# Moving the second out-projection's blocks beside the first top-k search, the latent projections beside attention, and the late scores behind it

## The chip, the cores and the metric

The kernel runs on one core of one Trainium2 chip. The metric is the device time of one execution in microseconds (us), lower is better, as the median of several runs. Five engines work in parallel, each through its own instruction queue in order: TensorE (PE: matmuls; PEld: its weight loads), VectorE (DVE), ScalarE (ACT), GpSimd (POOL) and SyncE (SP, which here only issues DMAs). POOL issues some DMAs too. They wait for each other by semaphores.

## The reference, cut to what matters

Two blocks run one after the other on x of 1024 positions x 1024 features. The first has a gated convolution mixer and a dilated attention mixer and ends in a norm. The second is the part that the change reorders:

```
h   = rmsnorm(x) * (1 + scale) + shift
c_q, c_kv, k_idx, w_idx = split(h @ w_in)            # 256 + 256 + 64 + 8 columns ("latents")
score = sum_h w_idx[h] * relu(q_idx[h] @ k_idx)      # per query over all earlier keys
sel   = top 256 keys of each query by score
o     = softmax(q_lat @ c_kv[sel] + bias) @ c_kv[sel] # 8 heads
x = x + gate * (o @ w_uv @ w_o)
x = x + gate2 * conv_ffn(norm(x))                    # 2816 hidden features
out = rmsnorm(x)
```

The top 256 are found as a mask: a bitwise search for the 256th largest score of each query, then -1e30 is added to what lies below. Attention is computed densely under that mask. Queries 0 to 255 need no search, since they have at most 256 keys.

## The kernel before, in words

The 1024 positions are two chunks (c = 0, 1) of 512. Activations lie with features on the partitions, so a tile is 128 x 512. Every float32 product is three matmuls, since each operand is split into a high and a low part (hi x hi, hi x lo, lo x hi): a block of 128 output features from 1024 inputs is 8 x 3 = 24 matmuls of 128x512 (`gemm`).

The Python function `emit` writes the program as generators that are stepped in an order written by hand: `take(gen, n)` steps one n times, `drive` runs it out, `alternate` steps several in turn, and `Steps` wraps one so that it can be stepped now and then (`go`) and finished (`finish`). A list scheduler then places the instructions on each engine's queue, in about the order written, and moves later work ahead where an engine would otherwise stand still. `tc.issue_after` pins instructions behind a given one. The order of each queue is therefore fixed when the program is built.

The stages around the change, in the order of before:

- **Out-projection of layer 1** (`finish_layer1`, two generators `ends1[0]`, `ends1[1]`, one per chunk): 8 blocks (k = 0 to 7) of 24 matmuls each, whose raw weights are split on ACT and POOL (L377, L378) and whose results DVE adds to x (L683); then the statistics of the norm (L419, L427, a broadcast matmul into PSUM) and its application on DVE (L448, L451), ACT and POOL (L385), which gives H2 of that chunk. Before, six of chunk 1's eight blocks are issued ahead of `project(0)` (`take(ends1[1], 6)`), so they stand while chunk 0's norm is applied.
- **`project(c)`**: four latent blocks and one block of 72 columns, each of 24 matmuls, then 24 matmuls for the indexer's queries: 144 matmuls. DVE splits parts of the results (L1147, L1170), norms them (L1120) and so on. Its weights come ready-made from DRAM (L372) into `wring`, three slots that all weights share.
- **`scores(t)`** for query tiles t of 128 queries. Each head and each piece of up to 512 keys takes two matmuls into one PSUM bank, a relu on ACT (L1231) and a multiply-add on DVE (L1233 for head 0, L1236 for the others). t = 2, 3 come early. t = 4 to 7 are `late_scores`: 64 pieces, with the relu's result in two buffers (`ring`) and their PSUM in the tag `mm`, which has three banks at that point and serves `keys` and the out-projections too.
- **`topk`**, the search: 32 counts per tile, on DVE (L1268) or ACT (L1265), each followed by small decisions on DVE (L1274, L1277, L1288), then the mask (L1299 to L1314, POOL L1316, L1318). The *first search* (tiles 3 on DVE and 2 on ACT) is stepped beside the last two blocks of chunk 1's out-projection, `keys(0)` and `project(1)`. The *second search* (4, 5 on DVE; 6, 7 on ACT) is pinned behind the last DVE and ACT instructions of chunk 0's attention and runs beside `finish_dsa(0)` and `ffn_in(0)`.
- **`keys(c)`**: 16 tiles of 6 matmuls, each split by ACT (L1180) and DVE (L1181) and stored (L1182).
- **`attention(0, masks)`**: per head a query (L1349, L1350) with keys and values loaded by POOL-issued DMAs (L1353, L1354), four logit tiles (DVE L1395 adds the mask and takes the maximum, ACT L1400 the exponential, DVE L1402, L1403 the normalisation), then transposes on PE (L1420), split by ACT L1424 and DVE L1425, and the product with the values (ACT L1439). Logits and transposes use the PSUM tag `ps`. In the text written, the scores of tiles 4, 5 come ahead of it and 6, 7 behind it.
- **`finish_dsa(0)`**: chunk 0's last out-projection (8 blocks), its norm, and behind it **`ffn_in(0)`**: 44 blocks of 24 matmuls, that cover the second search on PE, then run beside `attention(1)`.

The lines that the change touches are:

```
        take(ends1[1], 6)
        for gen in ends1[1], keys(0), project(1):
                for _ in range(min(left, 4)):
        late_scores((4, 5))
        searches = [Steps(topk(sc[0:2])), Steps(topk(sc[2:4], True))]
        attention(0, masks)
        late_scores((6, 7))
```

Of the kernel before, what the change touches and what calls it, by code (L numbers as in the profile page):

```python
# [200 lines left out]
def emit(tc, I, OUT):  # L201
# [14 lines left out]
    with sp as sp, pp as pp, dp as dp:  # L216
# [266 lines left out]
        def alternate(*gens):  # L483
            gens = [iter(g) for g in gens]
            while gens:
                for g in list(gens):
                    try:
                        next(g)
                    except StopIteration:
                        gens.remove(g)  # L490
# [8 lines left out]
        def take(gen, n):  # L499
            for _ in range(n):  # L500
                next(gen)
# [564 lines left out]
        take(ends1[0], 5)  # L1066
        load_y(yscr, Yc, 1)
        drive(ends1[0])
        take(ends1[1], 6)

        banks["ps"].append(banks["mm"].pop(0))
        banks["po"].append(banks["mm"].pop(0))
# [372 lines left out]
                dma(yscr2[h, :, CH(c)], y.f)  # L1445
            y.free()

        def attention(c, masks):

            state = {}  # L1450
            query = lambda h: head_query(c, h, state) if h < HEADS else ()
            front = lambda h: head_front(c, h, masks, state) if h < HEADS else ()
            if c == 0:
                for h in range(LOOK):
                    drive(query(h))
                drive(front(0))
                for h in range(HEADS):
                    alternate(front(h + 1), head_back(c, h, state), query(h + LOOK))
            else:
                drive(query(0))  # L1460
                drive(front(0))
                for h in range(HEADS):
                    alternate(chain(query(h + 1), front(h + 1)), head_back(c, h, state))
            for i in range(2):
                for b in cq[i][c]:
                    b.free()
# [130 lines left out]
            qs[h][0].free()  # L1597
        search = [Steps(topk(sc[1:])), Steps(topk(sc[:1], True))]
        left = 32
        for gen in ends1[1], keys(0), project(1):  # L1600
            for _ in gen:
                for _ in range(min(left, 4)):
                    left -= 1
                    for x in search:
                        x.go()
# [1 line left out]
            for x in search:  # L1607
                x.go()
        masks = {3: search[0].value[0], 2: search[1].value[0]}
        sc = [ar.new(128 * (t + 1)) for t in (4, 5, 6, 7)]  # L1610
        ring = [ar.new(512) for _ in range(2)]

        def late_scores(ts):
            for t in ts:
                drive(scores(t, "mm", sc[t - 4], ring))
            if 7 in ts:
                for h in range(HEADS):
                    qs[h][1].free()
                for b in [kh, kl] + ring:
                    b.free()  # L1620

        late_scores((4, 5))
        searches = [Steps(topk(sc[0:2])), Steps(topk(sc[2:4], True))]

        attention(0, masks)
        late_scores((6, 7))
        rest = keys(1)
        take(rest, 8)
# [40 lines left out]
```

## Time and profile before

| | us |
|---|---|
| three runs | 2771.68, 2781.21, 2783.33 |
| their median | 2781.21 |
| the profiled execution's own time | 2774.49 |
| its span in the profile | 2772.8 |
| PE busy | 2604.5 (94%) |
| DVE busy | 1520.8 (55%) |
| ACT busy / POOL busy | 1123.9 / 1011.4 |

PE is the engine with the most work, so the share of busy time says little by itself: what matters is where PE stands still or runs at the lower of its two clocks, and which engine it then waits for. All times of the trace are counted from the start of the span. A "busy" figure of a stretch counts the time in which at least one instruction ran; instructions of one engine overlap a little at their ends, so the durations of single ones add up to more.

### The profile page before, as it was taken

What the parts mean: (1) busy time and instruction counts of PE and PEld (TensorE: products, weight loads), DVE (VectorE), ACT (ScalarE), POOL (GpSimd) and SP (SyncE); (2) the same over time, 40 slices, a digit from 0 to 9 for tenths busy, and PEclk for the clock granted to TensorE, in tenths of its full rate; (3) what the DMA queues carried; (4) which work ended last, traced back from release to release, by engine and by line L of the source; (5) the groups of instructions that cost most, each with busy time, mean ns of one, the idle gap of its engine ahead of it and who ended that gap; (6) DMA issues with size and microseconds to landing.
All of it is one profiled execution on the core that took longest, in us unless ns stands there. A gap on an engine that the chain in (4) does not pass through costs nothing. (4 is left out here: it accounts for less than half of the span.)

```text
span 2772.8 us, 34023 instructions
## 1 busy us (share of the span) xinstructions
PE 2604.5 (94%) x12070; PEld 2144.7 (77%) x12070; DVE 1520.8 (55%) x3260; ACT 1123.9 (41%) x1936; POOL 1011.4 (36%) x770
## 2 busy tenths in 40 slices
PE   8998998879999999999989887899999999999998
PEld 7876886658888888888778766778788777888887
DVE  7787223332666656756666598899655541222211
ACT  4211224323455455545443556775434433111132
POOL 1122335414465356545536335221311155200053
PEclk9999999989999999999999989999999999999999
DMA  7477228854444444444335573687566664576632
GB/s 290 164 266 244 82 89 313 302 193 136 172 176 151 168 161 174 145 175 170 132 120 172 194 253 111 211 259 251 205 210 206 236 200 121 195 257 243 234 117 73
DMA packets 208582, 524.67 MB, mean 189 GB/s; under 512 B 22258, under 2 KB 82202, under 8 KB 192796
## 3 DMA queue, kind: packets, MB, share of 16 engines
q1 hardware_dynamic: 199052, 497.20, 52.0%
q0 software_dynamic: 9216, 25.17, 3.0%
q8 instruction: 95, 1.56, 0.2%
q14 instruction: 75, 0.61, 0.1%
q10 hardware_dynamic: 144, 0.14, 0.0%
HBM read 394.03 MB, written 129.97 MB: 189 GB/s over the span
## 5 line engine op out<-in xcount | busy, mean ns | idle before, releaser
L256 PE MATMUL p<-page,wring 128*128 128x512 f32 (+2 forms) x8586 | 2027.1, 394 | 66.3 <-ACT page L384 8.5
L256 PEld LDWEIGHTS p<-page,wring 128*128 128x128 f32 (+1 forms) x8586 | 1605.0, 190 | 417.5 <-issue 12.5
L256 PE MATMUL p<-page,page 128*128 128x512 f32 (+5 forms) x2811 | 587.5, 351 | 81.5 <-ACT page L384 19.7
L256 PEld LDWEIGHTS p<-page,page 128*128 128x128 f32 (+1 forms) x2811 | 465.6, 199 | 168.7 <-ACT page L384 21.1
L378 POOL TENSOR_TENSOR wring<-wraw,wring 128x1024 fp32r<-128x1024 f32 (+1 forms) x159 | 390.4, 2457 | 512.1 <-ACT wring L377 508.3
L377 ACT ACTIVATE wring<-wraw 128x1024 fp32r<-128x1024 f32 (+1 forms) x159 | 164.7, 1037 | 333.0 <-PE p L256 292.1
L385 POOL TENSOR_TENSOR page<-page,page 128x512 fp32r<-128x512 f32 (+1 forms) x87 | 130.7, 1510 | 402.7 <-ACT page L384 382.6
L384 ACT ACTIVATE page<-page 128x512 fp32r<-128x512 f32 (+1 forms) x136 | 86.7, 651 | 222.3 <-DMA page<-d 96.7
L736 POOL TENSOR_TENSOR page<-page,page 128x512 f32<-128x512 f32 x96 | 124.7, 1303 | 115.8 <-ACT page L735 113.9
L355 DVE TENSOR_TENSOR wraw<-wraw,page 128x1024 fp32r<-128x1024 f32 (+1 forms) x64 | 83.1, 1298 | 105.2 <-ACT page L354 85.2
L301 DVE SCALAR_TENSOR_TENSOR page<-page,page 128x1024 f32<-128x1024 f32 x88 | 114.0, 1295 | 33.4 <-DMA page<-wmod 33.0
L745 POOL TENSOR_TENSOR page<-page,page 128x512 fp32r<-128x512 f32 x64 | 103.8, 1623 | 62.1 <-ACT page L744 61.9
L1541 DVE SCALAR_TENSOR_TENSOR page<-p,page,page 128x512 f32<-128x512 f32 (+1 forms) x17 | 12.2, 719 | 201.9 <-PE p L256 201.9
L743 DVE TENSOR_TENSOR page<-page 128x512 f32<-128x512 f32 x64 | 95.4, 1492 | 25.6 <-POOL page L736 25.6
L738 DVE TENSOR_TENSOR page<-p,page 128x512 f32<-128x512 f32 x96 | 66.2, 689 | 78.3 <-ACT page L735 73.0
L354 ACT ACTIVATE page<-wraw 128x1024 fp32r<-128x1024 f32 (+1 forms) x64 | 67.3, 1052 | 86.1 <-DMA wraw<-w3i 36.6
L1265 ACT ACTIVATE page<-page,page 128x1024 bf16<-128x1024 f32 (+1 forms) x93 | 86.7, 933 | 32.4 <-DVE page L1288 29.0
L441 POOL TENSOR_TENSOR page<-page,page 128x512 f32<-128x512 f32 x40 | 54.6, 1365 | 98.2 <-ACT page L440 98.2
L744 ACT ACTIVATE page<-page 128x512 fp32r<-128x512 f32 x64 | 57.1, 892 | 76.0 <-DVE page L743 75.9
L1375 POOL TENSOR_TENSOR page<-page,page 128x256 f32<-128x256 f32 x64 | 47.8, 759 | 107.2 <-DMA d<-page 35.1
L734 ACT ACTIVATE page<-p 64x512 f32<-64x512 f32 x96 | 57.3, 596 | 70.3 <-PE p L256 46.1
L1268 DVE TENSOR_SCALAR_CACHE_REDUCE page<-page,page 128x768 bf16<-128x768 f32 (+1 forms) x93 | 81.5, 876 | 1.5
(213 smaller groups left out, 2273.4 us busy)
## 6 DMA issues: line engine op xcount, KB each, us to landing
wring<-d SPq DMA_DIRECT2D x122, 1024.0 KB, 5.4
d<-page SPq DMA_DIRECT2D x95, 512.0 KB, 3.1
page<-wmod SPq DMA_DIRECT2D x88, 512.0 KB, 4.3
d<-page SPq DMA_DIRECT2D x153, 256.0 KB, 4.2
d<-wraw SPq DMA_DIRECT2D x63, 512.0 KB, 3.3
page<-d SPq DMA_DIRECT2D x121, 256.0 KB, 3.2
wraw<-w1i SPq DMA_DIRECT2D x56, 512.0 KB, 3.3
wraw<-w3i SPq DMA_DIRECT2D x44, 512.0 KB, 3.5
```

Of the source, the lines that this page charges most:

```text
L256: lastn["mm"] = T.matmul(out, lhsT=l, rhs=r, start=start, stop=stop)
L301: V.scalar_tensor_tensor(w.f, w.f, 1.0, sil[j // 6].f, op0=OP.mult, op1=OP.mult, accum_out=m)
L355: V.tensor_sub(raw.r[:, :n], raw.f[:, :n], hi.f[:, :n])
L377: A.activation(hi.r[:, :n], raw.f[:, :n], AF.Copy)
L378: (lo_engine or G).tensor_sub(lo.r[:, :n], raw.f[:, :n], hi.f[:, :n])
L384: A.activation(hi.r[:, :n], src, AF.Copy)
L385: (engine or V).tensor_sub(lo.r[:, :n], src, hi.f[:, :n])
L736: G.tensor_mul(sw.f, sw.f, rope[1].f[:, CH(c)])
L743: V.tensor_tensor(a.f, a.f, sw.f, op=OP.add)
L745: G.tensor_sub(out[1], shape(a.f), out[2])
L1265: A.activation(junk.b[:, 0:sc.n], sc.f, AF.Sign, scale=-1.0, bias=at, accum_out=one)
L1268: V.tensor_scalar(junk.b[:, 0:sc.n], sc.f, at, None, op0=OP.is_ge, op1=OP.add, accum_out=one)
```

## The change

It changes four things in the order in which the program is written, and no computation:

1. `take(ends1[1], 2)` in place of 6: only two of chunk 1's out-projection blocks stand ahead of `project(0)`, and six behind it.
2. The first search is stepped beside those six blocks and `keys(0)`, twice per step of these instead of four times. `project(1)` is no longer in that list.
3. `project(1)` is handed to `attention(0)`, which steps it once after each head and then finishes it.
4. `late_scores((4, 5))` and the creation of the second search move behind `attention(0)`, next to `late_scores((6, 7))`.

```diff
-        take(ends1[1], 6)
+        take(ends1[1], 2)
...
-        def attention(c, masks):
+        def attention(c, masks, beside=None):
...
                 for h in range(HEADS):
                     alternate(front(h + 1), head_back(c, h, state), query(h + LOOK))
+                    beside.go()
+                beside.finish()
...
         left = 32
-        for gen in ends1[1], keys(0), project(1):
+        for gen in ends1[1], keys(0):
             for _ in gen:
-                for _ in range(min(left, 4)):
+                for _ in range(min(left, 2)):
...
         masks = {3: search[0].value[0], 2: search[1].value[0]}
-        sc = [ar.new(128 * (t + 1)) for t in (4, 5, 6, 7)]
-        ring = [ar.new(512) for _ in range(2)]
...
+        attention(0, masks, Steps(project(1)))
+        sc = [ar.new(128 * (t + 1)) for t in (4, 5, 6, 7)]
+        ring = [ar.new(512) for _ in range(2)]
         late_scores((4, 5))
         searches = [Steps(topk(sc[0:2])), Steps(topk(sc[2:4], True))]
-
-        attention(0, masks)
         late_scores((6, 7))
```

The scheduler turns this into queues. In the rows below, a line is "line, operation, what is written <- what is read, shape"; p_N is a PSUM tile, page_N a buffer, wring the weights.

**First place: PE's queue where chunk 0's norm is applied.** p_10550 is block k = 1 of chunk 1's out-projection, p_10583 block k = 2; p_10466 and p_10463 are the broadcasts of chunk 0's norm; p_10601, p_10628 and p_10674 are the first blocks of `project(0)`, which read H2 of chunk 0 (page_474, page_9764, ...). Before:

```order
L256 MATMUL p_10550<-page_3236,wring 128x512
L256 MATMUL p_10583<-page_1401,wring 128x512
L256 MATMUL p_10583<-page_3228,wring 128x512
L256 MATMUL p_10583<-page_1401,wring 128x512
L256 MATMUL p_10583<-page_1685,wring 128x512
L256 MATMUL p_10583<-page_3236,wring 128x512
L256 MATMUL p_10583<-page_1685,wring 128x512
L256 MATMUL p_10583<-page_9768,wring 128x512 x3
L256 MATMUL p_10583<-page_9769,wring 128x512 x2
L256 MATMUL p_10466<-page_10144,page_65 128x512
```

After the change:

```order
L256 MATMUL p_10550<-page_3236,wring 128x512
L256 MATMUL p_10466<-page_10144,page_65 128x512
L256 MATMUL p_10586<-page_9832,page_65 8x384
L256 MATMUL p_10463<-page_10137,page_65 128x512
L256 MATMUL p_10601<-page_474,wring 128x512
L256 MATMUL p_10628<-page_474,wring 128x512
L256 MATMUL p_10674<-page_474,wring 72x512
L256 MATMUL p_10601<-page_474,wring 128x512 x2
L256 MATMUL p_10601<-page_9764,wring 128x512 x3
L256 MATMUL p_10601<-page_6107,wring 128x512
```

The four blocks k = 2 to 5 (96 matmuls) that stood from here on are gone from this place, and three blocks that need the norm's results follow directly, interleaved.

**Second place: DVE's queue at the end of chunk 1's out-projection.** L683 takes a block's result, L1018 is its square sum, L1236 a score of tile 2 or 3, L1268 a count of the first search. Before, block k = 7 (p_11111):

```order
L1236 SCALAR_TENSOR_TENSOR page_9833<-page_10999,page_4249,page_9833 128x384
L683 SCALAR_TENSOR_TENSOR page_10184<-p_11111,page_65,page_10184 128x512
L1236 SCALAR_TENSOR_TENSOR page_11008<-page_11022,page_4249,page_11008 128x512
L1017 TENSOR_TENSOR page_10327<-page_10327,page_2664 128x512
L1018 SCALAR_TENSOR_TENSOR page_10327<-page_2664,page_65,page_10327 128x512
```

After the change, block k = 6 (p_11103):

```order
L683 SCALAR_TENSOR_TENSOR page_10867<-p_11103,page_65,page_10867 128x512
L1282 TENSOR_SCALAR page_4249<-page_4249 128x1
L1277 TENSOR_SCALAR page_4249<-page_4249 128x1
L1268 TENSOR_SCALAR page_9305,page_4249<-page_10876,page_4249 128x512
L1288 SCALAR_TENSOR_TENSOR page_4249<-page_4249 128x1
L1018 SCALAR_TENSOR_TENSOR page_10327<-page_10867,page_65,page_10327 128x512
L1274 TENSOR_SCALAR page_4249<-page_4249 128x1
```

Counts of the search now stand between the blocks. In the whole queue, ten of the 32 counts on DVE stand ahead of the first L448 of chunk 1's norm (none before), 23 ahead of the last L1181 of `keys(0)` (16 before), and the last is followed directly by attention.

**Third place: PE's queue at the scores of tiles 4 to 7.** L1420 are attention's transposes; what reads page_261 and page_2871 (the indexer's keys) is a score. Before, in the middle of attention:

```order
L256 MATMUL p_12763<-page_261,page_11457 128x512
L256 MATMUL p_12763<-page_2871,page_11457 128x512
L1420 MATMUL p_12354<-page_65,page_11815 128x128
L256 MATMUL p_12257<-page_10919,page_9764 128x384
L1420 MATMUL p_12354<-page_65,page_11796 128x128
L256 MATMUL p_12768<-page_261,page_11457 128x384
L256 MATMUL p_12768<-page_2871,page_11457 128x384
L256 MATMUL p_12773<-page_261,page_9769 128x512
L256 MATMUL p_12773<-page_2871,page_9769 128x512
L256 MATMUL p_12257<-page_10919,page_9764 128x384 x2
```

After the change, behind the last product of attention (p_12548):

```order
L256 MATMUL p_12548<-page_12145,page_10335 128x256 x2
L256 MATMUL p_12548<-page_12145,page_9764 128x256
L256 MATMUL p_12614<-page_261,page_1685 128x256
L256 MATMUL p_12614<-page_2871,page_1685 128x256
L256 MATMUL p_12619<-page_261,page_11434 128x384
L256 MATMUL p_12619<-page_2871,page_11434 128x384
L256 MATMUL p_12624<-page_261,page_11434 128x256
L256 MATMUL p_12624<-page_2871,page_11434 128x256
```

From here on 59 score tiles stand on PE's queue one behind the other with nothing between them, and the first eight tiles of `keys(1)` and then `finish_dsa(0)` behind those. On DVE's queue all 56 late L1236 stand behind attention's last L1425, with 14 counts of the second search among them and 4 more among the first eight L1181 of `keys(1)`; before, six counts stood ahead of the eighth of these L1181. Of `project(1)`, two latent blocks and the 72-column block stand ahead of attention's first transpose, the rest among its heads.

## Rows read from the trace of the kernel before

**Rows 1.** Page, part 2: busy tenths in 40 equal slices of the span

```profile
PE   8998998879999999999989887899999999999998
DVE  7787223332666656756666598899655541222211
PEclk9999999989999999999999989999999999999999
```

**Rows 2.** Stretches of the span by engine; header names the columns

```profile
core 0: us, PE busy (x) PEld busy (x) DVE busy (x) ACT busy (x) POOL busy (x), PEclk, DMA share, GB/s
...
1523.30:1585.70 62.40, 59.47 (x262) 47.21 (x261) 32.40 (x62) 30.82 (x58) 17.09 (x13) 0.95 0.56 203
1585.70:1621.90 36.20, 22.95 (x84) 17.22 (x83) 35.23 (x111) 27.24 (x59) 16.22 (x12) 0.76 0.73 245
1621.90:1662.50 40.60, 35.81 (x161) 27.53 (x160) 37.24 (x137) 21.64 (x51) 11.89 (x15) 0.96 0.73 248
1662.50:1777.00 114.50, 96.09 (x455) 75.09 (x454) 98.48 (x302) 76.45 (x181) 51.78 (x80) 0.91 0.41 123
1777.00:1854.50 77.50, 67.36 (x284) 54.32 (x283) 70.95 (x202) 59.37 (x106) 15.17 (x12) 0.95 0.90 292
1854.50:1946.00 91.50, 91.50 (x403) 75.91 (x403) 84.37 (x231) 51.69 (x87) 19.61 (x18) 0.99 0.68 229
1946.00:2206.00 260.00, 252.40 (x1263) 211.08 (x1262) 147.01 (x400) 113.02 (x193) 47.53 (x78) 1.00 0.65 219
```

**Rows 3.** PE in order of time, from chunk 0's norm on

```profile
1493.84 17.84 PE L256 MATMUL p<-page,wring 128*128 128x512 f32 x76
...
1531.81 2.88 PE L256 MATMUL p<-page,wring 128*128 128x512 f32 x8 [2.71 <-DMA wring<-d]
```

**Rows 4.** DVE in order of time: chunk 0's norm, first and last

```profile
1494.45 3.38 DVE L448 SCALAR_TENSOR_TENSOR page<-page,page,p 128x512 f32<-128x512 f32 x5 [2.41 <-PE p L256]
...
1509.71 0.74 DVE L451 SCALAR_TENSOR_TENSOR page<-page,page,page 128x512 fp32r<-128x512 f32 x1
```

**Rows 5.** PE in order of time: chunk 1's norm

```profile
1592.86 2.93 PE L256 MATMUL p<-page,wring 128*128 128x512 f32 x6 [4.91 <-DVE page L1274]
1603.94 4.86 PE L256 MATMUL p<-wring,page 128*128 128x512 f32 x12 [8.15 <-DVE page L1181]
```

**Rows 6.** DVE in order of time: two counts of the first search, its end

```profile
1616.20 0.75 DVE L1268 TENSOR_SCALAR_CACHE_REDUCE page<-page,page 128x512 bf16<-128x512 f32 x1
...
1617.37 0.75 DVE L1268 TENSOR_SCALAR_CACHE_REDUCE page<-page,page 128x512 bf16<-128x512 f32 x1
...
1650.67 0.75 DVE L1268 TENSOR_SCALAR_CACHE_REDUCE page<-page,page 128x512 bf16<-128x512 f32 x1
...
1662.05 0.75 DVE L1314 SCALAR_TENSOR_TENSOR page<-page,page,page 128x512 f32<-128x512 f32 x1
```

**Rows 7.** DVE groups of the stretch 1662.5 to 1777: busy, mean ns, idle before

```profile
L1236 DVE SCALAR_TENSOR_TENSOR page<-page,page,page 128x512 f32<-128x512 f32 (+2 forms) x56 | 40.7, 737 | 0.5 <-ACT page L1231 0.5
L1395 DVE CUSTOM_DVE_ANT_0 page<-p,page 128x256 f32<-128x256 f32 (+1 forms) x47 | 16.9, 374 | 6.7 <-PE p L256 4.0 <-POOL page L1375 2.5
...
L1350 DVE SCALAR_TENSOR_TENSOR page<-p,page 128x512 fp32r<-128x512 f32 x6 | 4.1, 686 | 5.1 <-ACT page L1349 5.1
L1233 DVE TENSOR_SCALAR page<-page,page 128x512 f32<-128x512 f32 (+2 forms) x8 | 4.0, 509 | 0.0
...
L1170 DVE TENSOR_TENSOR page<-p,page 64x512 fp32r<-64x512 f32 x2 | 1.4, 688 | 0.1
L1181 DVE TENSOR_TENSOR page<-p,page 128x512 fp32r<-128x512 f32 x2 | 1.4, 684 | 0.0
```

**Rows 8.** ACT group of the same stretch: the relus of the scores

```profile
L1231 ACT ACTIVATE page<-p,page 128x512 f32<-128x512 f32 (+2 forms) x64 | 37.7, 607 | 15.5 <-DVE page L1236 9.1 <-PE p L256 3.8 <-DVE page L1398 2.1
```

**Rows 9.** PE in order of time: start of chunk 0's last out-projection

```profile
1785.65 46.66 PE L256 MATMUL p<-page,wring 128*128 128x512 f32 x198 [4.04 <-DVE page L1181]
```

## The prediction, made before the result was known

> **What bounds the kernel now.** I read the page first. PE is in the nineties in most slices, but in slices 21 to 26, counted from one, it falls to 7 and 8 and its granted clock dips, while DVE goes to 8 and 9 [rows 1]. So the kernel is PE-bound on the whole, and DVE-bound for some 350 us around the first search and chunk 0's attention, which is what the change reorders. Next I read that stretch stage by stage, cut at events that both kernels have [rows 2]: out-projection of chunk 1 up to its norm (to 1585.7), that norm and `keys(0)` (to 1621.9), the end of the first search with `project(1)` (to 1662.5), chunk 0's attention with all late scores (to 1777), `finish_dsa(0)` (to 1854.5), `ffn_in(0)` over the second search (to 1946), and attention on chunk 1. The reader should see three things there. PE loses most in two stages: 36.2 us with 22.95 busy at a mean granted clock of 0.76 (a mixture of 1.2 and 2.4 GHz), and 114.5 us with 96.1 busy at 0.91. In the latter DVE is busy 98.5 us of 114.5, so DVE paces it. And in the first stage of the rows DVE is busy only 32.4 us of 62.4: it has room there. From 1854.5 to 1946 PE is busy without a gap although the second search is still running, so the end of that search holds nothing up.
>
> I therefore forecast when PE reaches one point that both kernels have with the same work behind it: the start of `finish_dsa(0)`'s out-projection, 1785.65 us in this trace, which runs PE solid [rows 9]. All sums are against this one execution (own time 2774.49 us); it lies 0.24% under the median of 2781.21, and I add the difference that I find to the median.
>
> **1. Chunk 0's norm loses its cover: +4 us.** Blocks k = 2 to 5 are gone from there. A matmul of 128x512 at 2.4 GHz takes 17.84 / 76 = 0.235 us [rows 3], so 96 of them were 22.6 us of cover. The norm on DVE runs from 1494.45 to 1510.45 [rows 4], 16 us, less the out-projection's own rows in it, some four of 0.7: 13 us. The three blocks of `project(0)` that now follow need H2, but plane by plane: 72 matmuls, 16.9 us, of which a third can be issued for each plane as it comes. I count some 3 us until the first plane and 1 us until later ones: 4. Bounds: 0 (planes always ahead) and 13 (nothing before the last plane). The 2.71 us for weights that come late [rows 3] stays as it is, since SP still issues the same transfers in the same neighbourhood.
>
> **2. The six blocks beside the scores of tiles 2, 3 and ten counts: 0.** The blocks only move; a count of the search takes 1617.37 - 1616.20 = 1.17 us of DVE with its small decisions [rows 6], so ten take 12 us, out of the 30 in which DVE stood idle before 1585.7 [rows 2]. That idle time is the cover; if DVE were late here, PE's next wait would be on `keys(0)`.
>
> **3. Chunk 1's norm and `keys(0)`: -3 us.** The stage is a DVE queue of 8 L448, 4 L451, the writes L1181 and counts; PE waits on it 4.91 and 8.15 us [rows 5]. It keeps all of them but has 13 counts instead of 16: 3 x 1.17 = 3.5.
>
> **4. The end of the first search: -19 us.** Behind the last write of `keys(0)` 9 counts are left, not 16. Nine take 10.5 us; from the last count at 1650.67 to the masks at 1662.5 there are 11.8 [rows 6], less some of `project(1)`'s L1170 (0.69 each [rows 7]) that no longer stand there: in all 21 to 22, against 40.6. PE is not starved: logits and the first three blocks of `project(1)` (72 matmuls, 17 us) stand there. So the masks are ready at 1662.5 + 4 - 3 - 19 = 1645 about. PE has some 17 us of `project(1)` still before it at that point; it is not ahead by 17 us, only DVE is.
>
> **5. Attention without scores: 80 us, not 114.5.** In the 114.5 us the scores hold 56 L1236 and 8 L1233, 44.7 us by their durations [rows 7]. Single rows overlap: five in 3.38 us are 0.68 each where one alone is 0.74 [rows 4]; taking 0.07 off each leaves 40. The rest of DVE is 98.5 - 40 = 58.5. Added are `project(1)`'s own: 6 L1170, 2 L1147, two L1120 and some of its norm, some 13 rows of 0.6: 8. Sum 66.5. At the same share of 98.5 / 114.5 = 0.86 that is 77. I take 80, as the filler is gone: the scores themselves waited for 0.5 us only, whereas attention's own rows waited 6.7 (L1395) and 5.1 us (L1350) [rows 7]. Bounds: 66.5 (DVE never waits) and 98 (the 16 us in which DVE idled come twice).
>
> **6. Late scores behind it: +55 us.** They keep their 40 us of DVE, with 14 counts of the second search among them, about 1.1 us each: 15. PE has only 128 matmuls there, 64 of 512, 32 of 384 and 32 of 256 columns, 64 x 0.235 + 32 x 0.18 + 32 x 0.12 = 25 us, so it stands idle for 30; the relus on ACT are 37.7 us and wait for DVE as the buffers are two [rows 8]. This is the price of the change: before, attention filled these gaps. Nothing else can: `keys(1)` and the out-projection take PSUM from the same three banks, and stand behind. Bounds 50 and 64 (DVE at 0.86 of the time).
>
> On the clock: when PE had waited 8.15 us, the next 12 matmuls took 4.86 us, 0.405 each, which is the 1.2 GHz level [rows 5]. At that pace the 128 score matmuls take 64 x 0.405 + 32 x 0.30 + 32 x 0.20 = 42 us, still under DVE's 55, so the clock costs nothing until `keys(1)`: 48 matmuls, 11 us or 19. The Trainium skill (TensorE: Matmul & The Clock Gate, section "A second HAM failure mode: psum-queue depth-cycling") says that a PE which cycles through PSUM banks with short idle times between groups loses throughput as its clock falls and recovers again. By that rule term 7 would be up to 8 us more and the result 2794; the trace has no run of scores alone to show it.
>
> **7. The first eight tiles of `keys(1)`: +12 us.** 48 matmuls, 11 us at 2.4 GHz; DVE has 8 L1181 (0.68 [rows 7], 0.6 net) and 4 counts, 9 us. Bounds 11 and 20.
>
> **8. Afterwards: -1.5 us.** 18 counts of the second search are behind by then rather than 6, so masks come earlier, but PE was covered [rows 2]. Of the 7.6 us that PE idles from 1946 to 2206 (260 - 252.4) I take a fifth.
>
> **The sum.** 1645 + 80 + 55 + 12 = 1792, against 1785.65: +6.4, less 1.5: **+5 us**, 2779.4 on the profiled execution's scale, **2786 us** on the median's. What DVE gains by searching early is spent by the scores standing alone.
>
> **Rivals.** 0.5% is 13.9 us, about what a measurement of this kernel can tell from no change: below 2767 is faster, above 2795 slower.
>
> *Faster: DVE never waits once the masks are there.* Attention and the scores are then two plain queues of DVE work: 66.5 + 50 + 11 behind 1645 gives 1772.5, -13; with the later gaps mostly returned (-6), -19: 2762. For it: DVE was at 0.9 and more in much of the old stage with worse mixing; against it: the waits of L1395 and L1350, which are waits on a chain through PE and ACT, not on throughput. It decides if the masks are followed by attention within about 70 us. 0.22.
>
> *Slower: attention(0) becomes bound by its chain.* Logit, maximum, exponential, normalisation, transpose, split and product of a head follow each other through three engines, with four banks for logits and transposes; the scores hid that. Then term 5 is 98, the end 1810, +24 less 1.5: 2804. For it: DVE's idle waits in rows 7 all belong to attention. Against: two heads alternate, and blocks of `project(1)` now stand between them for PE. It decides if attention takes over some 88 us after the masks. 0.32.
>
> *The reordering is a wash.* The scheduler pulls `project(1)` and logits to wherever PE is free anyway, so that only the order of the same DVE work changes and both extra waits and gains stay under a few us: 2781. This lies in the middle band with the forecast: 0.14, the forecast itself 0.32.
>
> **How the numbers follow.** Faster 0.22, same 0.32 + 0.14 = 0.46, slower 0.32. If all lower bounds met, the sum would be 1641 + 66.5 + 50 + 11 = 1768.5 and 2758; if all upper ones, far over 2820; eight in ten I put from 2762 (the faster rival) to 2810 (the slower with part of the clock's 8 us). The forecast's own range is 2774 to 2798.
>
> **What would show it.** In the changed profile: PE busy but for a few us while chunk 0's norm is applied (term 1); L1268 rows between L683 rows, and the last L1314 of the first search near 1645 (4); from there to the last L1425 of chunk 0 some 80 us (5); then a stretch of some 55 us with all L1236 in it, DVE busy almost throughout and PE idle for about half (6); the out-projection near 1792 (7); no PE gap where the second search ends. I am wrong if the masks come later than 1655, if scores still mix with attention on the chip, or if attention needs under 70 or over 90 us.

## The result and the profile after

The changed kernel takes 2813.89 us as the median of four runs (2810.74 to 2815.62), against 2776.44 us of the kernel before in the same series: a ratio of 1.0149, 95% interval 1.0122 to 1.0177. It is slower by 41 us by the ratio, 37 by the two medians. The forecast was 2786 us and the range ended at 2810. Differences in us that are given with a ratio below are worked out from it (ratio less 1, times the median of before in the same series). One run of e2 (4360.66 us) and one of e12 (4973.76 us) had a lower granted clock than the others (0.56 and 0.90, against 0.97 to 0.98) and are left out of the medians and ratios below.

The page of the changed kernel, part 2 (compare [rows 1]):

```profile
PE   8998998879999999999988878799999999999998
...
DVE  7787223432657656665674886898755442223211
...
PEclk9999998989999999999999988899999999999999
```

The weak stretch of PE is still in slices 21 to 26, at 8, 8, 8, 7, 8, 7 (before: 8, 9, 8, 8, 7, 8). DVE reads 7, 4, 8, 8, 6, 8, 9, 8, 7 in slices 21 to 29, where it read 6, 6, 5, 9, 8, 8, 9, 9, 6: it has a new low in the middle, and is busy longer.

Part of the difference between the two profiled executions (41 us) lies ahead of the change. The last L738 stands before the first moved instruction, in code that both kernels share: up to there their queues on PE, DVE, ACT and POOL hold the same instructions in the same order. In time order on DVE, of the kernel before:

```profile
1391.05 0.68 DVE L738 TENSOR_TENSOR page<-p,page 128x512 f32<-128x512 f32 x1
```

and of the changed kernel:

```profile
1402.84 0.68 DVE L738 TENSOR_TENSOR page<-p,page 128x512 f32<-128x512 f32 x1
```

So 11.8 us of the 41 lie ahead of all that the change moved. The other profiles say that this is scatter between executions: in the eleven (of 14) whose four queues are the same up to this row, it starts anywhere from 1386.5 to 1402.8. From here on I count from it. The end is then 1381.7 us behind it before and 1411.1 after: the change itself costs 29 us in these two executions.

The stretches of the changed kernel, cut at the events of [rows 2] (chunk 0's norm, chunk 1's norm, last L1181 of `keys(0)`, last L1314, last L1425 of chunk 0, last L1236, start of `finish_dsa(0)`, start of `ffn_in(0)`, end of the second search):

```profile
core 0: us, PE busy (x) PEld busy (x) DVE busy (x) ACT busy (x) POOL busy (x), PEclk, DMA share, GB/s
1502.20:1612.20 110.00, 96.80 (x407) 74.78 (x408) 72.89 (x158) 55.05 (x109) 38.56 (x25) 0.94 0.48 170
1612.20:1650.90 38.70, 21.84 (x72) 15.97 (x72) 36.30 (x100) 25.79 (x55) 18.05 (x15) 0.69 0.74 242
1650.90:1673.30 22.40, 19.43 (x86) 14.79 (x85) 19.68 (x74) 3.49 (x10) 10.54 (x17) 0.96 1.13 366
1673.30:1769.70 96.40, 81.92 (x393) 64.88 (x392) 69.00 (x243) 50.04 (x131) 42.09 (x70) 0.89 0.43 133
1769.70:1830.60 60.90, 45.38 (x139) 26.41 (x138) 53.93 (x110) 41.31 (x73) 6.61 (x7) 0.80 0.09 31
1830.60:1838.20 7.60, 7.60 (x35) 6.17 (x34) 7.57 (x22) 6.73 (x13) 0.46 (x1) 1.00 0.87 262
1838.20:1907.00 68.80, 62.56 (x266) 50.03 (x265) 65.45 (x198) 56.40 (x99) 12.33 (x10) 0.95 0.93 320
1907.00:1981.00 74.00, 74.00 (x332) 61.52 (x331) 60.67 (x163) 42.66 (x71) 14.95 (x16) 1.00 0.72 247
```

Three things are to be seen. The end of the first search fell from 40.6 to 22.4 us, as meant. What was 114.5 us of attention with scores became 96.4 of attention and 60.9 of scores. And in those 96.4 us no engine is near its limit: DVE is busy for 69, PE for 82.

A second view of the same thing, the lengths of stages in all kernels of this study, worked out from the times of single rows in each trace (us; "first" is the last L738 to chunk 0's first L448; "blocks" from there to chunk 1's first L448; "keys" to the end of the last L1181 of `keys(0)`; "search" to the end of the last L1314; "attention" to the end of chunk 0's last L1425; "rest" to the first L683 of `finish_dsa(0)`; "tail" to the end):

```
           first blocks  keys search attention  rest   tail  whole
before     103.4   91.3  36.2   40.8     113.0  22.1  974.8 1381.7
changed     99.4  110.0  38.7   22.5      96.3  74.7  969.5 1411.1
e1          99.3  110.1  36.0   30.9     124.0  19.1  976.6 1396.0
e2         101.7   91.2  38.8   31.0      88.1  75.7  976.1 1402.5
e3         103.4   91.3  36.3   40.9     113.7  21.8  974.7 1381.9
e4         100.8  110.8  38.2   25.3     107.9  36.9  973.2 1393.2
e5          98.2  110.7  35.2   32.2     114.5  19.1  969.3 1379.2
e6         102.9   89.6  36.2   40.6      87.1  78.1  985.0 1419.5
e7          99.8  110.1  38.7   23.2      99.2  69.7  975.8 1416.5
e8         101.0   89.9  37.1   36.2     134.2  28.3  978.4 1405.1
e9          99.6  102.4  41.1   33.7     113.3  19.9  964.3 1374.2
e10        100.5  113.6  38.1   24.7     105.1  41.8  965.2 1389.0
e11        103.2  100.4  38.6   30.3     107.6  23.0  970.9 1373.9
e12        102.1   46.5  63.6   69.3      91.3  22.4  963.4 1358.7
```

The changed kernel against before: the masks come at the same time (270.5 us behind the common row, and 271.7), since the out-projection takes 15 us more, `keys(0)` 2 more and the end of the search 18 less. From the masks to the out-projection it is 171.0 instead of 135.1 us, 36 more; the tail gives 5 back.

### The profile page after: what moved, and what is told of

Its sections match the earlier page's. It is cut to its first block, busy times and chain, and to the rows that moved or that the text cites. A ratio compares the mean times of both kernels' runs of the same rounds, so it can differ in the third digit from the quotient of the medians.

```text
span 2813.9 us, 34065 instructions
## 1 busy us (share of the span) xinstructions
PE 2631.3 (94%) x12070; PEld 2155.4 (77%) x12070; DVE 1533.4 (54%) x3260; ACT 1135.6 (40%) x1944; POOL 1002.8 (36%) x770
## 5 line engine op out<-in xcount | busy, mean ns | idle before, releaser
L256 PE MATMUL p<-page,page 128*128 128x512 f32 (+5 forms) x2803 | 601.8, 357 | 90.2 <-ACT page L384 18.9
L738 DVE TENSOR_TENSOR page<-p,page 128x512 f32<-128x512 f32 x96 | 66.1, 689 | 79.0 <-ACT page L735 73.6
L1511 ACT ACTIVATE page<-p 128x512 f32<-128x512 f32 x44 | 26.2, 596 | 148.3 <-PE p L256 148.3
L1517 DVE TENSOR_SCALAR page<-page,page 128x512 f32<-128x512 f32 x44 | 27.8, 632 | 104.5 <-ACT page L1511 104.5
```

The costliest lines, as they stand in the source:

```text
L256: lastn["mm"] = T.matmul(out, lhsT=l, rhs=r, start=start, stop=stop)
```

## The experiments

Theory M says that the loss comes from taking attention and late scores apart: each alone is bound by its own chain or by DVE, and together they filled each other's waits. Theory O says that it comes from the out-projection, where the search now stands among the blocks. Theory P, in later expectations, says that `project(1)` beside attention costs by itself. Every ratio below is against the kernel before, run on the same chip in the same series.

**e1: the first two parts alone.**

```diff
-        take(ends1[1], 6)
+        take(ends1[1], 2)
...
-                for _ in range(min(left, 4)):
+                for _ in range(min(left, 2)):
```

> Only the first two parts of the change: two blocks ahead of project(0), six beside the first search, two steps of the search per block instead of four; project(1) and the late scores stay where they were before. Theory M (the cost is in the lost mixture): chunk 1's norm starts about 15 us later than before (as in the changed kernel, once the 12 us that its profile already had at 1400 us are taken off), but the masks come about 18 us sooner after the last write of keys(0), and attention still has project(1) and the scores to mix with: the time is within 8 us of before. Theory O (the cost is in the out-projection, where the search now holds up its results): the 15 us stay and the time is 12 to 20 us above before.

2787.86 us, ratio 1.0048 (1.003 to 1.0066), 13 us: just over what M allowed, inside O's. The blocks are 15 us later, as in the changed kernel.

**e2: the last two parts alone** (the changed kernel with `take(ends1[1], 6)` and four steps).

> Only the last two parts: project(1) beside attention and the late scores behind it; the out-projection stands as before (six blocks ahead, four steps of the search per block). Theory M: attention alone takes some 96 us and the scores behind it some 61 us, as in the changed kernel, against 114.5 us together before; some 10 us of DVE work leave the end of the search with project(1), and some 10 us are given back behind the out-projection: 20 to 30 us above before. Theory O: with the out-projection as before, the time is within 8 us of before.

2805.58 us, 1.0102 (1.0057 to 1.0147): 28 us, as M expected. The two halves add up to the whole change (13 + 28 = 41, with intervals of 8 to 18, 16 to 41 and 34 to 49). It also shows that the sooner masks were worth nothing: in e2 the search ends 31.0 us behind `keys(0)`, in the changed kernel 22.5, but the sum of "search" and "attention" is 119.1 and 118.8.

**e3: only the scores of tiles 4 and 5 written behind attention.**

```diff
-        late_scores((4, 5))
-        searches = [Steps(topk(sc[0:2])), Steps(topk(sc[2:4], True))]
         attention(0, masks)
+        late_scores((4, 5))
+        searches = [Steps(topk(sc[0:2])), Steps(topk(sc[2:4], True))]
         late_scores((6, 7))
```

> Only the scores of tiles 4 and 5 (and with them the second search) written behind attention; project(1) stays beside the first search. Theory M: attention with nothing beside it takes 85 to 96 us, the scores alone about 60 us, and the time is 20 to 35 us above before. Theory O: within 8 us of before. If the scheduler still pulls the scores of 4 and 5 in between the heads, the time is that of before under both.

2774.63 us, 1.0003 (0.9985 to 1.0021), and the stages of before: the scheduler does pull the scores forward. On PE, DVE, ACT and POOL all instructions stand in the order of before, so e3 is a second measurement of that kernel and puts neither theory to the test. What it shows is that the place of the late scores in the text costs nothing. In the changed kernel they can't be pulled, because their inputs come from `project(1)`, which is stepped beside the heads there and finishes with them. Its last step splits the queries that the scores read (L1170 on DVE); the first and the last of the eight in the changed kernel:

```profile
1746.96 0.68 DVE L1170 TENSOR_TENSOR page<-p,page 64x512 fp32r<-64x512 f32 x1
...
1759.41 0.69 DVE L1170 TENSOR_TENSOR page<-p,page 64x512 fp32r<-64x512 f32 x1
```

So no late score could begin in the first 74 us of attention (1673.3 to 1769.7). In the kernel before these splits run from 1653.8 to 1668.8, around the end of the search at 1662.5. That is the part which takes the mixture away.

**e6: the mixture alone taken away**, `project(1)` staying beside the first search.

```diff
-        late_scores((4, 5))
+        attention(0, masks)
+        with tc.issue_after(ends[V].ins), tc.issue_after(ends[A].ins):
+            late_scores((4, 5))
         searches = [Steps(topk(sc[0:2])), Steps(topk(sc[2:4], True))]
-
-        attention(0, masks)
...
```

(and `late_scores((6, 7))` in the same way)

> The kernel before, with the late scores held behind chunk 0's attention on DVE and ACT (project(1) stays beside the first search). Theory M (the mixture is worth its whole overlap): from the masks attention takes 85 to 95 us, the scores behind it 55 to 62 us, so the out-projection comes 25 to 40 us later than in the kernel before and the time is 20 to 35 us above it. Theory P (project(1) beside attention is what costs): the time stays within 10 us of before.

2814.18 us, 1.014 (1.0108 to 1.0172): 39 us, a little over M's range, for this edit alone. In its profile the first result of the out-projection comes 28 us later than before (434.5 us behind the common row, and 406.9), as M expected; the other 10 lie in the tail (985.0 and 974.8), and no run shows where they come from. Its stretches of attention and of scores:

```profile
1665.00:1752.20 87.20, 62.69 (x299) 45.33 (x298) 60.65 (x234) 43.05 (x115) 44.35 (x76) 0.96 0.46 137
1752.20:1815.00 62.80, 46.38 (x142) 26.09 (x141) 54.57 (x112) 41.56 (x74) 5.82 (x7) 0.84 0.07 25
```

Attention by itself takes 87 us with PE busy 63, DVE 61, POOL 44 and ACT 43: no engine is the bound, which leaves the chain of waits from engine to engine (argued from these figures, not tested by itself). The scores take 63 with DVE at 55.

**e4: the changed kernel with the mixture given back.** The scores are stepped beside the heads directly behind `project(1)`:

```diff
+        def beside():
+            yield from project(1)
+            for t in (4, 5, 6, 7):
+                yield from scores(t, "mm", sc[t - 4], ring)
...
-        attention(0, masks, Steps(project(1)))
+        attention(0, masks, Steps(beside()))
...
-                    beside.go()
+                    beside.go(6)
```

> The changed kernel, but with the late scores stepped beside attention's heads again, directly behind project(1) (six steps per head). Theory M: attention and scores take together about 115 to 125 us rather than 157, and the time falls by 25 to 40 us from the changed kernel's, to within 10 us of before. Theory O: the time stays within 10 us of the changed kernel's.

2790.5 us, 1.005 (1.0032 to 1.0068): 14 us above before, so 27 of the 41 are gone. From the masks to the out-projection 26 of the 36 lost us come back:

```profile
1671.40:1779.30 107.90, 92.81 (x480) 74.60 (x481) 92.03 (x289) 73.77 (x180) 49.36 (x75) 0.97 0.41 124
1779.30:1816.30 37.00, 29.59 (x112) 20.37 (x111) 36.45 (x88) 27.24 (x47) 3.65 (x4) 0.91 0.45 148
```

That is M's fall, though it was to end within 10 us of before. The scores still begin late, behind `project(1)`, and 37 us of them are left over.

**e7: six buffers for the relu's results in place of two** (`ring = [ar.new(512) for _ in range(6)]` in the changed kernel).

> The changed kernel with six buffers for the relu's results of the late scores instead of two. Theory R (relu and multiply-add wait for each other over two buffers): the stretch of scores falls from 61 us to about 54, the DVE work in it, and the time by 5 to 8 us. Theory D (DVE is the bound there): the stretch stays within 2 us and so does the time.

2810.32 us, 1.0128 (1.0089 to 1.0166). That is 6 us less than the changed kernel, but the two intervals overlap. "Rest" falls from 74.7 to 69.7 and attention is 2.9 longer. Two buffers may cost a few us of that stretch and no more; what fills it is DVE's work.

**e8: the mixture with the first search as before** (e4 with `take(ends1[1], 6)`, four steps, and `beside.go(8)`).

> Project(1) beside attention and the late scores stepped behind it beside the heads (eight steps per head), with the out-projection and the search's paces as before. Theory M: with the mixture back and the out-projection undisturbed nothing is left of the loss: within 6 us of before, 10 to 16 us under the run that mixes but keeps the first two parts. Theory P: project(1) beside attention costs by itself, 10 us or more above before.

2798.18 us, 1.0083 (1.0051 to 1.0116), 23 us above before: M missed, P was right. The masks are early here, yet the out-projection comes 162.5 us behind them, as in e2 without any mixture (163.8). PE's queue shows two long waits:

```profile
1658.60 4.18 PE L256 MATMUL p<-page,page 128*128 128x512 f32 x12 [23.20 <-issue]
...
1688.84 1.86 PE L256 MATMUL p<-page,page 128*128 128x1 f32 x8 [9.87 <-POOL page L441]
```

In the first, most of it ahead of the masks (1654.2), PE stands still with `project(1)` undone; what it waits for there the trace doesn't name. e2, the other run with `project(1)` beside attention and the first search as before, has such a wait too:

```profile
1667.72 2.90 PE L256 MATMUL p<-page,page 128*128 128x512 f32 x6 [19.47 <-issue]
```

In both it ends 0.1 us behind the third L1395 at the masks, here of e8:

```profile
1658.06 0.43 DVE L1395 CUSTOM_DVE_ANT_0 page<-p,page 128x256 f32<-128x256 f32 x1
```

and of e2:

```profile
1667.19 0.42 DVE L1395 CUSTOM_DVE_ANT_0 page<-p,page 128x256 f32<-128x256 f32 x1 [0.33 <-POOL page L1375]
```

L1395 reads logits out of the tag `ps`. So it is likely that logits held its banks until the masks were there, and PE's queue stood behind the next tile that needed one; no run tests it. The second row of e8 is a square sum of `project(1)`'s norm, which waits for POOL while attention's products and the scores stand behind it on the same queue. What a filler waits for, everything behind it waits for.

**e10: e4 with four steps of the search per block.**

> The run that mixes project(1) and the late scores with attention (it was 14 us above before), with four steps of the search per block instead of two. Theory Q (the pace of two is what is left of the loss, since the first two parts with a pace of four cost nothing): within 5 us of before. Theory P (project(1) beside attention has a price of its own): still 10 us or more above before.

2783.52 us, 1.0032 (1.0011 to 1.0054): 9 us above before (3 to 15), between the two and nearer P. `project(1)` beside attention keeps a price of its own also when the scores are mixed in.

**e5: two blocks ahead, four more between `project(0)` and the search, all else as before.**

```diff
-        take(ends1[1], 6)
+        take(ends1[1], 2)
...
+        take(ends1[1], 4)
         left = 32
```

> The kernel before with only two blocks of chunk 1's out-projection ahead of project(0) and four more between it and the search, so that the first search is stepped as before. It holds only the lost cover at chunk 0's norm. Theory N (in the first part of the change the cover costs): PE waits some 5 us there, chunk 1's norm starts 5 us later, and the time is 4 to 7 us above before. Theory S (the search beside the blocks costs, since its counts and its small decisions hold up the blocks' results on DVE): the same 5 us, and the run of the first two parts alone, 13 us above before, has some 8 us more than this one. If this one is 10 to 15 us above before, the search costs nothing and it is all cover.

2774.82 us, 1.0007 (0.9986 to 1.0028): no difference, where each of the three expectations had at least 4 us. The edit doesn't hold only the cover, though: the scheduler put eleven counts ahead of chunk 1's norm here as well, so the blocks are as late as in e1. They are late in both, and only e1 is slower. So late blocks need not cost anything by themselves. What e1 has besides is the pace of two: behind the masks, which come at the same time in both (276.4 and 276.3), its attention takes 124 us and not 114.5, and its tail 7 us more; why, I can't say.

**e9: the counts held behind the last block's result on DVE,** to part the cover from the counts.

```diff
-                V.scalar_tensor_tensor(xo.f, p, gate[:, k:k + 1], xo.f, op0=OP.mult, op1=OP.add)
+                added[0] = V.scalar_tensor_tensor(xo.f, p, gate[:, k:k + 1], xo.f, op0=OP.mult, op1=OP.add)
...
-        take(ends1[1], 6)
+        take(ends1[1], 2)
...
+        drive(ends1[1])
         left = 32
-        for gen in ends1[1], keys(0), project(1):
+        for gen in keys(0), project(1):
...
+                    with tc.issue_after(added[0].ins):
```

> As the run with two blocks ahead and four between project(0) and the search, but here all six blocks come before the search and the counts on DVE are held behind the last result of the blocks (L683), which the scheduler had not done in that run: it had put 11 counts ahead of chunk 1's norm there too. Theory S (counts hold up the last blocks' results): the last result follows PE's last product within 2 us instead of 8, and chunk 1's norm starts 7 to 10 us later than in the kernel before instead of 15, from the same point of the first layer. Theory N (the cover and nothing else): still 13 to 16 us later. The search then ends later behind keys(0); the time is within 8 us of before under both.

2775.22 us, 1.0008 (0.999 to 1.0026). Chunk 1's norm comes 7.3 us later than before instead of 14.7, as Theory S expected: half of the delay is the cover and its neighbourhood, half the counts. The parting isn't complete, as six counts still stand ahead of that norm (ten in the changed kernel). Here too the later blocks cost nothing in the whole. PE at chunk 0's norm, in time order:

```profile
1500.18 1.18 PE L256 MATMUL p<-page,wring 128*128 128x512 f32 x3 [2.73 <-ACT page L450]
1504.04 8.32 PE L256 MATMUL p<-page,wring 128*128 128x512 f32 x28 [2.68 <-DVE page L451]
```

and DVE at the last two blocks (L685 here is L683):

```profile
1585.69 0.74 DVE L685 SCALAR_TENSOR_TENSOR page<-p,page,page 128x512 f32<-128x512 f32 x1
...
1587.89 0.75 DVE L685 SCALAR_TENSOR_TENSOR page<-p,page,page 128x512 f32<-128x512 f32 x1
```

The two results are 2.2 us apart; in the changed kernel, 6.4 (below).

**e11: four blocks ahead in place of six; e12: all eight.** These go on with the question that e5 raised, whether the place of the blocks matters at all, and in which direction.

```diff
-        take(ends1[1], 6)
+        drive(ends1[1])
...
-        for gen in ends1[1], keys(0), project(1):
+        for gen in keys(0), project(1):
```

(e12; e11 has `take(ends1[1], 4)` only)

> The kernel before with four blocks ahead of project(0) instead of six, nothing else. If moving the blocks pays at the end of the search and costs at the norm in the same amount, as with two blocks ahead, the time is within 4 us of before; if the cover of two blocks is enough for the norm, it keeps the gain of some 8 us behind keys(0) and is 3 to 8 us under before.

2771.11 us, 0.9989 (0.9968 to 1.001): the same as before.

> The opposite of the change: all eight blocks of chunk 1's out-projection ahead of project(0), the search beside keys(0) and project(1) as before. Chunk 1's norm can then start early, beside project(0), but nothing is left to cover the scores of tiles 2 and 3. If the early norm counts, keys(0) comes sooner and the time is 5 to 12 us under before; if PE stands still at the scores instead, 0 to 10 us above.

2759.01 us, 0.9927 (0.9901 to 0.9953): 20 us under before, more than expected, and under every kernel of this study. It does the opposite of the change's first part. Its stretches from chunk 0's norm on (then chunk 1's norm, end of `keys(0)`, masks, end of attention, first L683):

```profile
1497.90:1544.50 46.60, 46.60 (x210) 36.63 (x209) 30.47 (x43) 16.21 (x25) 23.30 (x14) 1.00 0.58 197
1544.50:1608.00 63.50, 56.66 (x242) 43.66 (x241) 49.24 (x97) 46.59 (x92) 25.39 (x20) 0.95 0.70 247
1608.00:1677.30 69.30, 56.03 (x229) 40.28 (x228) 64.12 (x230) 39.85 (x95) 19.23 (x24) 0.86 0.71 226
1677.30:1768.60 91.30, 80.64 (x397) 61.79 (x397) 84.22 (x274) 65.03 (x156) 43.90 (x71) 0.96 0.41 124
```

Chunk 1's norm falls into the time in which DVE had room, 46 us after chunk 0's, with `project(0)` to cover it on PE. `keys(0)` and `project(1)` are done sooner, so that late scores begin before the masks (the fifteenth L1236, the first late one, is at 1660.3; the masks are at 1677.3). The masks come 10 us later than before, from the common row, and the out-projection 12 us sooner (395.2 and 406.9). Another 11 us of this profile's gain lie in the tail (963.4 and 974.8), and no run shows where they come from. Counting from the common row is less exact for e12, since its queues on PE and DVE differ from the others' from some 65 us ahead of that row.

## Why the prediction was wrong

Two steps of the prediction failed: term 2, which put the six blocks beside the counts at nothing, and the step from the masks on, which let attention's 80 us (term 5) start at the masks. The sum put the start of the out-projection on PE 6 us later. In the changed kernel the eight key tiles are the first 48 matmuls of this row, so it starts at 1838.2:

```profile
1827.12 22.65 PE L256 MATMUL p<-page,wring 128*128 128x512 f32 x96
```

Less the 11.8 us ahead of the common row that is 1826.4, against 1785.65: 41 later, or 39 if one allows for the key tile that still stands in the row of [rows 9]. By its first result on DVE, the point of the table above, it came 35 later (441.5 us behind the common row and 406.9), of which 5 came back. Two groups of terms were too small by about 16 us each; term 6 was 6 too small and term 7 gave 4 back. Two of the signs of being wrong that I had named came: masks later than 1655 (1673.4 less 11.8 is 1661.6), and attention over 90 us.

**Terms 1 to 3: forecast +1, measured +17** (14.7 for the blocks, 2.4 for `keys(0)`). Term 1 is close: PE waits 2.74 and 2.55 us at chunk 0's norm, 5 for the 4 forecast. Term 2, costed at nothing, is the one that failed; term 3, put at -3, is the 2.4, and no run shows why. PE in the changed kernel, at chunk 0's norm and at the end of the blocks:

```profile
1503.72 1.31 PE L256 MATMUL p<-page,wring 128*128 128x512 f32 x3 [2.74 <-ACT page L450]
1507.58 2.93 PE L256 MATMUL p<-page,wring 128*128 128x512 f32 x6 [2.55 <-DVE page L451]
...
1593.87 1.67 PE L256 MATMUL p<-page,wring 128*128 128x512 f32 x6 [0.86 <-DVE page L1282]
1600.25 2.93 PE L256 MATMUL p<-page,wring 128*128 128x512 f32 x6 [4.71 <-DVE page L683]
```

and DVE at the same place:

```profile
1590.66 0.74 DVE L1236 SCALAR_TENSOR_TENSOR page<-page,page,page 128x512 f32<-128x512 f32 x1
...
1591.97 0.69 DVE L1268 TENSOR_SCALAR_CACHE_REDUCE page<-page 128x512 bf16<-128x512 f32 x1
...
1593.06 0.75 DVE L683 SCALAR_TENSOR_TENSOR page<-p,page,page 128x512 f32<-128x512 f32 x1
...
1597.02 0.74 DVE L1268 TENSOR_SCALAR_CACHE_REDUCE page<-page,page 128x512 bf16<-128x512 f32 x1
...
1599.45 0.75 DVE L683 SCALAR_TENSOR_TENSOR page<-p,page,page 128x512 f32<-128x512 f32 x1
```

I had counted ten counts into the 30 us in which DVE stood idle before chunk 1's norm. But a count needs all scores of its tile: the last L1236 of tile 3 ends at 1591.4, and the first count on DVE follows at 1592. From the common row that is 189 us, against 198 before. The idle time had gone by when the counts could start (DVE stood idle for 31.5 us from chunk 0's norm to 1565, for 4.5 to 1592, and for 1.1 from there to chunk 1's norm at 1612.2), so they came into the one place where the blocks' last results, the statistics and the norm follow each other, and the results wait behind them. Cover must lie where the work can run, not only be large enough. e9 gives the size: 7.4 of the 14.7 us. Terms 1 to 3 are why the masks come at 1661.6 (11.8 us taken off) and not at the 1645 of the forecast. It isn't shown that the late blocks cost time of their own: e5 and e9 have them, and take as long as before.

**Term 4: forecast -19, measured -18.3.** Right, and worth nothing. The step from the masks to the end was wrong: I took attention to start its count of 80 us at the masks. From the end of `keys(0)` to the end of attention it is 119 us in the changed kernel and in e2 alike, whose masks are 8.5 us apart. PE is busy for 101 of them (19.43 + 81.92), with much of `project(1)` in its queue.

**Term 5: forecast 80, measured 96.4**, near the upper bound of 98. DVE's work was counted right (66.5; busy 69). Its waits, in the groups of that stretch, were not:

```profile
L1395 DVE CUSTOM_DVE_ANT_0 page<-p,page 128x256 f32<-128x256 f32 (+1 forms) x46 | 16.3, 379 | 12.6 <-PE p L256 11.6 <-POOL page L1375 0.7
L1425 DVE TENSOR_TENSOR page<-p,page 128x512 fp32r<-128x512 f32 (+3 forms) x32 | 15.0, 485 | 4.8 <-ACT page L1424 4.6
...
L1402 DVE RECIPROCAL page<-page 128x1 f32<-128x1 f32 x31 | 4.7, 157 | 3.8 <-ACT page L1400 3.5
...
L1350 DVE SCALAR_TENSOR_TENSOR page<-p,page 128x512 fp32r<-128x512 f32 x6 | 4.1, 690 | 4.0 <-ACT page L1349 4.0
```

In the kernel before L1395 waited 6.7 us and L1350 5.1 [rows 7]; the other two:

```profile
L1425 DVE TENSOR_TENSOR page<-p,page 128x512 fp32r<-128x512 f32 (+3 forms) x32 | 15.0, 481 | 2.5 <-ACT page L1424 2.4
...
L1402 DVE RECIPROCAL page<-page 128x1 f32<-128x1 f32 x32 | 4.8, 153 | 0.8 <-ACT page L1400 0.8
```

So all but L1350 wait longer now, L1395 most of all. DVE stands idle for 27 us of 96.4 here, and stood idle for 16 of 114.5 with the scores beside it. PE's own waits in this stretch are for `project(1)`'s steps above all:

```profile
PE p L256 <- ACT page L1156: 4.1, 1, 4.1
PE p L256 <- DVE page L1120: 2.4, 1, 2.4
PE p L256 <- DVE page L1170: 1.6, 2, 1.2
```

So the slower rival had the right sign and for this term nearly the right price, in part by luck: it named attention's own chain alone, and e6 shows 87 us for that. The other 9 have no run of their own. `project(1)` in the queue isn't enough to explain them, since e2 has it too and takes 88, from masks that come 8.5 us later behind `keys(0)`.

**Term 6: forecast 55, measured 60.9**, within its bounds. DVE sets it, as argued, with little waiting:

```profile
L1236 DVE SCALAR_TENSOR_TENSOR page<-page,page,page 128x512 f32<-128x512 f32 (+2 forms) x56 | 35.5, 670 | 4.3 <-ACT page L1231 4.3
L1268 DVE TENSOR_SCALAR_CACHE_REDUCE page<-page,page 128x640 bf16<-128x640 f32 (+1 forms) x12 | 11.3, 941 | 0.1
```

**Term 7: forecast 12, measured 7.6** behind the last score, as a few matmuls of these tiles had run beside the last scores. The granted clock fell to 0.80 in the scores' stretch and was 1.00 in the next, so the 8 us that a slower clock could have cost did not come. (The twelve matmuls from which I took the price of 1.2 GHz ran at a mean granted clock of 0.59, so they were a mixture of both levels.) By the rule that I weighed there from the Trainium skill (TensorE: Matmul & The Clock Gate, section "A second HAM failure mode: psum-queue depth-cycling"), a PE that cycles through banks with short waits loses clock: the 0.80 agrees with it, but DVE was the bound and nothing hung on it.

**Term 8: forecast -1.5, measured -5.3**, where the tails of all kernels lie between 963 and 985. Whether that is scatter or order isn't shown: before and e3, whose queues are the same, differ by 0.2 us, and the order in the tail differs from kernel to kernel.

**The price that I gave to the right thing.** I wrote that the scores standing alone is the price of the change, and put it at 55 + 80 + 12 = 147 against 123, 24 us; from the masks to the same point it was 96.4 + 60.9 + 7.6 = 165, 42 us (36 by DVE's first result). What I held against it, the sooner masks, brought nothing. The text also laid the loss of the mixture to the order in which late scores are written; e3 shows that this order is free and that `project(1)` takes it away.

Open stay what in the pace of two makes e1's attention 10 us longer than e5's, what PE waited for in e8's 23 us (banks are likely, not tested), and why `project(1)` beside attention keeps a price when the scores are mixed in. The 29 us between the two profiles lie under the interval of the ratio (34 to 49 us). Each kernel has one profile, whose scatter ahead of the common row was left out and whose tail differs by up to some 20 us for reasons that aren't shown, so I read the stages from the profiles and the whole from the ratio.

## What to carry to other kernels

Two stages that run mixed, each with waits in its own chain, can take much less time together than one behind the other: before you part them, add the lengths that each has alone, not the work of the busiest engine (here 87 + 63 against 113 together). Look for what ties a filler to its place: not the line where it is written, if a scheduler may pull it, but the producer of its inputs. And free time of an engine is cover only from the moment at which the moved work has its inputs; here moving the norm into that free time (e12) gained 20 us, of which the stages up to the out-projection show 12, where moving the search towards it gained nothing.

## What the runs showed of the hardware that was not expected

The same instructions on the same queues took from 1386.5 to 1402.8 us up to the last L738 in eleven profiles, a scatter of 16 us before the part under study; behind that row two profiles with the same queues repeat most stages within tenths of a us ("blocks" 91.3 and 91.3, "keys" 36.2 and 36.3, "search" 40.8 and 40.9, "attention" 113.0 and 113.7 in before and e3). Counting from a row that all kernels share is what made differences of a few us readable.
